# Output projection as seven block products over summed weights, with x tiles of equal rows

## The chip, the cores and the metric

The kernel runs on one core of a Trainium2 chip. The metric is the device time of one launch in microseconds (us). Most of the work is TensorE's (PE in the profile, PEld for its weight loads); VectorE (DVE) and ScalarE (ACT) prepare operands and evacuate results, GpSimd (POOL) and SyncE (SP) issue transfers.

## The reference

One layer of a hybrid encoder, 512 tokens and 16 learned meta tokens, width 2048, all in float32:

```python
hn = rmsnorm(h, norm_pre_w)
proj = hn @ w_in                       # 2048 -> z, xbc, dt, q, k, v, gate
y   = rmsnorm_groups(ssd(conv(xbc), dt) * silu(z))     # 2048 columns
att = banded_sink_attention(q, k, v) * silu(g_att)     # 1024 columns
out = concat([y, att]) @ w_out         # (512 x 3072) @ (3072 x 2048)
h = h + rmsnorm(out, norm_post_w)
```

The change concerns the last product, `out`, and what leads up to it.

## The kernel before

Every large product is made in float32 by splitting each operand into a rounded part and a remainder (`hi` and `lo` for weights, `mh` and `ml` or `xh` and `xl` for activations) and adding three matmuls: hi with high, hi with low, lo with high. A weight chunk of 128 x 1024 numbers (512 KB) is loaded by SP into a tile `st` (two of them), cast to `hi` by ScalarE (L132) and subtracted to `lo` by VectorE (L133), three tiles of each. `use(n)` on L137 asks for chunk n: it splits up to chunk n+2 and loads ahead of that. A tile of `hi` can be written again only when the matmuls of the chunk three before it are done.

The program has three stages. In the input projections (L157) 68 column tiles are multiplied, each with two chunks; the normalised x lies transposed in 16 tiles `xh[k]` and 16 `xl[k]`, grouped by four k with rows of 640, 576, 544 and 528 numbers (`X_ROW`), of which 528 are used. The 32 projections without meta tokens read 512 columns, the others two pieces of 272 (or 260) and 256. First come keys, values, and eight pairs of query and gate projections with the attention (`attend`, L512) between them; then eight groups with convolution and state-space work. Work between projections is written as generators: `yield d` means that the next part is emitted d us of estimated TensorE time later. A scheduler turns the emitted program into one order per engine, and each engine runs its own in that order; it may place a ready instruction or DMA far ahead of its place in the code.

The output projection (L853 to L905) goes over four column blocks of 512. Each takes 12 weight chunks; a chunk serves 24 matmuls (two k tiles, four token tiles, three terms), 4 x 12 x 24 = 1152 in all, each with 512 columns. Activations are split once (`splitting`, L779). A finished block is squared by ScalarE (`ojk`, L894) and weighted by VectorE (L895) straight from PSUM; after the last block `finish` (L839) takes the root and its reciprocal, and for each token tile adds the residual (L850) and stores four blocks.

Of the kernel before, what the change touches and what calls it, by code (L numbers as in the profile page):

```python
# [7 lines left out]
F32 = mybir.dt.float32  # L8
F32R = mybir.dt.float32r
# [18 lines left out]
NST = 2  # L28

X_ROW = (640, 576, 544, 528)  # L30
# [13 lines left out]
def hybrid_layer(ctx, tc, x, pre, npre, w_in, w_dt, par, w_out, npost, cst, out):  # L44
    nc = tc.nc

    def sb(name, bufs=1, **kw):
        return tc.tile_pool(name=name, bufs=bufs, **kw)
# [13 lines left out]
    def bank(pool, name):  # L62
        return pool.tile([P, 512], F32, tag="b", name=name)
# [6 lines left out]
    cw = cpool.tile([P, 32, 4], F32, name="cw")  # L70
# [39 lines left out]
    NCH = NCI + 4 * (NKO // 2)  # L110
    staged, ready = {}, {}
    nload, nsplit = [0], [0]

    def load(upto):
        while nload[0] < min(upto, NCH):
            n = nload[0]
            st = wpool.tile([P, 1024], F32, tag="st", bufs=NST, name=f"st{n}")
            if n < NCI:
                src = w_in[n // 2, :, 1024 * (n % 2):1024 * (n % 2 + 1)]
            else:  # L120
                src = w_out[(n - NCI) // (NKO // 2), (n - NCI) % (NKO // 2)]
            nc.sync.dma_start(st, src)
            staged[n] = st
            nload[0] += 1
# [58 lines left out]
    with sb("pro", side="right") as pp:  # L183
# [116 lines left out]
        with tc.manual_schedule(engines={ET.PE, ET.Activation, ET.DVE, ET.Pool}):  # L300
# [59 lines left out]
            nc.vector.tensor_scalar(cw.rearrange("p a b -> p (a b)"), pr[:, P_CW:P_CW + P], 0.5, None, ALU.mult)  # L360
# [25 lines left out]
    def steps():  # L386
# [42 lines left out]
        en = sp.tile([P, P], F32, name="en")  # L429
# [5 lines left out]
        ec = sp.tile([P, P], F32, name="ec")  # L435
# [37 lines left out]
    def keys(t, pieces):  # L473
        kr = ap.tile([P, T], F32, tag="kr", bufs=1, name=f"kr{t}")
        rope(pieces, kr, f"k{t}")
        for hh in range(2):
            src = kr[64 * hh:64 * hh + 64, :]
            g = 2 * t + hh
            own = kh[64 * hh:64 * hh + 64, g, :]
            for half in (hh, 1 - hh):  # L480
                rows = slice(64 * half, 64 * half + 64)
                nc.scalar.activation(kh[rows, g, :], src, AF.Copy, scale=0.125)
            for half in range(2):
                rows = slice(64 * half, 64 * half + 64)
                nc.vector.scalar_tensor_tensor(kl[rows, g, :], src, 0.125, own.bitcast(F32),
                                               ALU.mult, ALU.subtract)
# [14 lines left out]

    keys(0, pieces0)
# [9 lines left out]
    def attend(hp, pieces):  # L512
# [10 lines left out]
        yield 10.0  # L523
# [34 lines left out]
        yield 9.0  # L558
# [36 lines left out]
        m = mapool.tile([P, S], F32, tag="m", bufs=8, name=f"ma{hp}")  # L595
        nc.vector.scalar_tensor_tensor(m, av, 0.5, gates[hp], ALU.mult, ALU.mult)
        mix[hp] = m
# [12 lines left out]
    ub = [vpool.tile([P, T + 3], F32, name=f"ub{i}") for i in range(2)]  # L610
# [22 lines left out]
    pools = {}  # L633
# [54 lines left out]
    def unit_task(u_, xs, cT):  # L688
# [84 lines left out]
        nc.vector.reciprocal(sq, sq)  # L773
        for v, yt in ((u_ - 1, y0), (u_, yy)):
            m = pools["y"].tile([P, S], F32, tag="m", bufs=16, name=f"my{v}")
            nc.vector.scalar_tensor_tensor(m, yt, hw[:, v:v + 1], sq, ALU.mult, ALU.mult)
            mix[8 + v] = m

    def splitting(ks):  # L779
        for k in ks:  # L780
            mh[k] = o_pool(k).tile([P, S], F32R, name=f"mh{k}")
            ml[k] = o_pool(k).tile([P, S], F32R, name=f"ml{k}")
            nc.scalar.copy(mh[k], mix[k])  # L783
            nc.vector.tensor_tensor(ml[k], mix[k], mh[k].bitcast(F32), ALU.subtract)
# [31 lines left out]
    mh, ml = [None] * NKO, [None] * NKO  # L816
    vpool.release()
    xpool.release()
    o1 = ctx.enter_context(sb("o1", reuse_waits="tile"))
    o2 = []  # L820
    xr = [None] * NT

    def o_pool(k):
        if k < 16:
            return o1
        if not o2:
            assert not tasks
            pools["s"].release()
            o2.append(tc.alloc_tile_pool(name="o2", bufs=1, side="right", reuse_waits="tile"))
        return o2[0]  # L830

    with tc.high_priority(offset=400):
        splitting([0, 1])
    npw = ssq = None
    ot = {}
    n3 = None
    NC = NKO // 2

    def finish(t, jk):  # L839

        b = 3
        rs = o1.tile([P, 2], F32, tag="ors", bufs=4, name=f"ors{t}")
        nc.vector.tensor_reduce(rs[:, 0:1], ssq[:, t, 0:3], AX.X, ALU.add)
        nc.vector.tensor_scalar(rs[:, 0:1], rs[:, 0:1], 1.0 / D, EPS, ALU.mult, ALU.add)
        nc.scalar.activation(jk, pss[t], AF.Square, accum_out=ssq[:, t, 3:4])
        nc.scalar.activation(rs[:, 1:2], ssq[:, t, 3:4], AF.Sqrt, bias=rs[:, 0:1], scale=1.0 / D)
        nc.vector.tensor_tensor(ot[b, t], pss[t], npw[:, b * 512:(b + 1) * 512], ALU.mult)
        nc.vector.reciprocal(rs[:, 1:2], rs[:, 1:2])
        for b in range(4):
            nc.vector.scalar_tensor_tensor(ot[b, t], ot[b, t], rs[:, 1:2], xr[t][b], ALU.mult, ALU.add)  # L850
            nc.sync.dma_start(out[t * P:(t + 1) * P, b * 512:(b + 1) * 512], ot[b, t])

    for r in range(4):  # L853
        b = r
        toks = range(NT)
        pool = wk if b % 2 else pj
        pss = {t: bank(pool, f"po{b}_{t}") for t in toks}
        order = []
        last = 3 if r == 3 else 1
        for c in range(NC - last):  # L860
            order += [(c, kk, t) for kk in range(2) for t in toks]
        order += [(c, kk, t) for t in toks for c in range(NC - last, NC) for kk in range(2)]
        held = {}
        for c, kk, t in order:
            if c not in held:
                held[c] = use(NCI + r * NC + c)
                if r == 0 and 2 * c + 3 < NKO:
                    splitting([2 * c + 2, 2 * c + 3])
            hi, lo = held[c]
            k = 2 * c + kk  # L870
            cs = slice(t * P, (t + 1) * P)
            wh, wl = hi[:, kk * 512:(kk + 1) * 512], lo[:, kk * 512:(kk + 1) * 512]
            if n3 is None and nload[0] == NCH and b == 3:
                n3 = xr[3] = []
                for b2 in range(2):
                    xq = wpool.tile([P, 1024], F32, tag="st", bufs=NST, name=f"xr3_{b2}")
                    nc.sync.dma_start(xq, x[3 * P:, b2 * 1024:(b2 + 1) * 1024])
                    xr[3] += [xq[:, 0:512], xq[:, 512:1024]]
            for i, (a, w_) in enumerate(((mh, wh), (mh, wl), (ml, wh))):
                nc.tensor.matmul(pss[t], a[k][:, cs], w_, start=(k == 0 and i == 0), stop=(k == NKO - 1 and i == 2))  # L880
            tick(0.648)
            if k == NKO - 1:
                if npw is None:
                    npw = o1.tile([P, D], F32, name="npw")
                    ssq = o1.tile([P, NT, 4], F32, name="ssq")
                    nc.sync.dma_start(npw, npost.partition_broadcast(P))
                mp, nb = (mapool, 8) if b < 2 else (pools["y"], 16)
                o = mp.tile([P, S], F32, tag="m", bufs=nb, name=f"o{b}_{t}")
                jk = o1.tile([P, S], F32, tag="jk", bufs=1, name=f"ojk{b}_{t}")
                ot[b, t] = o  # L890
                if b == 3:
                    finish(t, jk)
                    continue
                nc.scalar.activation(jk, pss[t], AF.Square, accum_out=ssq[:, t, b:b + 1])  # L894
                nc.vector.tensor_tensor(o, pss[t], npw[:, b * 512:(b + 1) * 512], ALU.mult)  # L895
        if r == 2:
            xr[0] = o1.tile([P, D], F32, name="xr0")
            nc.sync.dma_start(xr[0], x[0:P, :])
            xr[0] = [xr[0][:, b2 * 512:(b2 + 1) * 512] for b2 in range(4)]
            for t in (1, 2):  # L900
                xr[t] = []
                for b2 in range(4):
                    xq = pools["y"].tile([P, S], F32, tag="m", bufs=16, name=f"xr{t}_{b2}")
                    nc.sync.dma_start(xq, x[t * P:(t + 1) * P, b2 * 512:(b2 + 1) * 512])
                    xr[t].append(xq)  # L905
    o2[0].release()
# [70 lines left out]
```

## Time and profile before

| | |
|---|---|
| time, median of 3 runs | 1207.39 us (1205.78 to 1208.28) |
| the profiled execution | 1206.65 us, of which its span 1204.9 us |
| mean granted TensorE clock | 0.998 |
| busy: PE / DVE / ACT / POOL | 99% / 56% / 37% / 4% of the span |
| DMA | 125.5 MB, mean 104 GB/s |

Busy time of PE overlaps between one matmul and the next, so its pace is read from the starts of matmuls, not from their lengths. DMA share is the mean busy share of 16 DMA engines. A window's row names its stretch, its length, and for each engine the busy us and the number of instructions.

### The profile page before, as it was taken

The numbers are of one execution on the slowest core, as the hardware profiler recorded it, in microseconds if no ns is written. First come the engines' busy times: TensorE is split into PE (matmuls) and PEld (weight loads), VectorE is DVE, ScalarE is ACT, GpSimd is POOL, SyncE is SP. The second block draws the span as 40 slices with busy tenths as digits, with TensorE's granted clock in tenths as the row PEclk, the third lists the DMA queues.
The fourth block names the chain that finished last, engine by engine and source line by source line (L and its number), as shares of the span: only waits on it lengthen the run. The fifth ranks groups of instructions, "written<-read, shape, count | busy, mean of one in ns | idle before, by whom it ended". The sixth has DMA issues, their size and how long they took to land.

```text
span 1204.9 us, 18243 instructions
## 1 busy us (share of the span) xinstructions
PE 1192.1 (99%) x7565; PEld 1058.1 (88%) x7565; DVE 676.4 (56%) x1196; ACT 442.8 (37%) x754; POOL 48.5 (4%) x84
## 2 busy tenths in 40 slices
PE   8999999999999999999999999999999999999997
PEld 6998888888999989999999899998998788888886
DVE  7655555555556766656658557576675922222325
ACT  7544544445422423424234233242332712121212
POOL 0000000000100001010000000100100000000000
PEclk9999999999999999999999999999999999999999
DMA  6332222222323233233333232323332423233534
GB/s 228 100 97 88 71 86 73 71 76 91 115 95 111 91 106 99 96 108 104 105 98 97 95 116 88 114 86 105 109 97 70 157 88 104 92 101 94 169 101 179
DMA packets 37045, 125.53 MB, mean 104 GB/s; under 512 B 4706, under 2 KB 5346, under 8 KB 36706
## 3 DMA queue, kind: packets, MB, share of 16 engines
q1 hardware_dynamic: 32864, 111.78, 28.5%
q0 software_dynamic: 4096, 12.59, 3.3%
q8 instruction: 59, 0.97, 0.3%
q14 instruction: 24, 0.19, 0.1%
q10 hardware_dynamic: 2, 0.01, 0.0%
HBM read 120.03 MB, written 4.33 MB: 103 GB/s over the span
## 4 chain that ended last, share of the span: by engine, by line
PE 98%; DMA 1%; DVE 0%; ACT 0%; SPq 0%; issue 0%; DVEq 0%
PE pa L157 48%; PE po L880 22%; PE pb L157 17%; PE yd L722 1%; PE av L590 1%; PE stp L732 1%; PE yo L745 1%; PE ptp L572 1%; PE xt L228 1%; PE sc L542 1%; PE cbp L649 1%; DMA x<-in_x 1%; PE xp L702 1%; PE sc L541 1%; PE stp L730 1%; PE warm L278 0%
## 5 line engine op out<-in xcount | busy, mean ns | idle before, releaser
L133 DVE TENSOR_TENSOR lo<-st,hi 128x1024 fp32r<-128x1024 f32 x182 | 222.7, 1224 | 379.9 <-ACT hi L132 376.7
L157 PE MATMUL pa<-xh,hi 128*128 128x272 f32 (+2 forms) x1088 | 374.7, 344 | 0.0
L157 PE MATMUL pa<-xl,hi 128*128 128x272 f32 (+2 forms) x1088 | 366.1, 336 | 0.0
L157 PE MATMUL pa<-xh,lo 128*128 128x272 f32 (+2 forms) x1088 | 365.8, 336 | 0.0
L132 ACT CAST hi<-st 128x1024 fp32r<-128x1024 f32 x182 | 191.4, 1052 | 471.6 <-PE po L880 169.0
L157 PEld LDWEIGHTS pa<-xh,hi 128*128 128x128 f32 x1088 | 205.5, 189 | 24.5 <-issue 3.9
L157 PEld LDWEIGHTS pa<-xh,lo 128*128 128x128 f32 x1088 | 205.4, 189 | 21.4
L157 PEld LDWEIGHTS pa<-xl,hi 128*128 128x128 f32 x1088 | 205.3, 189 | 19.0
L157 PE MATMUL pb<-xh,lo 128*128 128x256 f32 x576 | 162.6, 282 | 0.0
L157 PE MATMUL pb<-xl,hi 128*128 128x256 f32 x576 | 162.4, 282 | 0.0
L157 PE MATMUL pb<-xh,hi 128*128 128x256 f32 x576 | 162.3, 282 | 0.0
L880 PE MATMUL po<-hi,mh 128*128 128x512 f32 x384 | 149.5, 389 | 1.2 <-ACT mh L783 1.2
L880 PE MATMUL po<-lo,mh 128*128 128x512 f32 x384 | 149.4, 389 | 0.0
L880 PE MATMUL po<-hi,ml 128*128 128x512 f32 x384 | 148.9, 389 | 0.0
L157 PEld LDWEIGHTS pb<-xh,hi 128*128 128x128 f32 x576 | 108.5, 188 | 1.1
L157 PEld LDWEIGHTS pb<-xl,hi 128*128 128x128 f32 x576 | 108.4, 188 | 0.0
L157 PEld LDWEIGHTS pb<-xh,lo 128*128 128x128 f32 x576 | 108.4, 188 | 0.0
L880 PEld LDWEIGHTS po<-hi,mh 128*128 128x128 f32 x384 | 72.1, 188 | 16.2 <-ACT mh L783 1.4
L880 PEld LDWEIGHTS po<-lo,mh 128*128 128x128 f32 x384 | 72.1, 188 | 15.0
L880 PEld LDWEIGHTS po<-hi,ml 128*128 128x128 f32 x384 | 72.1, 188 | 15.0
L626 DVE SCALAR_TENSOR_TENSOR cv<-ub,cw,cv 128x528 f32<-128x528 f32 (+1 forms) x96 | 73.4, 764 | 2.4
L627 ACT ACTIVATE ct<-cv 128x528 f32<-128x528 f32 (+1 forms) x32 | 20.5, 641 | 67.1 <-DVE cv L626 67.0
(210 smaller groups left out, 1067.6 us busy)
## 6 DMA issues: line engine op xcount, KB each, us to landing
st<-in_w_in SPq DMA_DIRECT2D x136, 512.0 KB, 3.7
st<-in_w_out SPq DMA_DIRECT2D x48, 512.0 KB, 3.5
R<-scr POOLq DMA_DIRECT2D x32, 256.0 KB, 3.6
x<-in_x SPq DMA_DIRECT2D x8, 512.0 KB, 9.4
ev<-scr POOLq DMA_DIRECT2D x32, 128.0 KB, 3.0
out<-o SPq DMA_DIRECT2D x16, 256.0 KB, 2.4
xr<-in_x SPq DMA_DIRECT2D x8, 256.0 KB, 6.6
npw<-in_npost SPq DMA_DIRECT2D x1, 1024.0 KB, 4.4
```

The costliest lines, as they stand in the source:

```text
L132: nc.scalar.copy(hi, st)
L133: nc.vector.tensor_tensor(lo, st, hi.bitcast(F32), ALU.subtract)
L157: nc.tensor.matmul(ps, wt, xt[k][:, a:b], start=(k == 0 and j == 0), stop=(k == NKT - 1 and j == 2))
L228: nc.tensor.transpose(tp[:, kk, :], xts[j][:, k * P:(k + 1) * P], ident)
L541: nc.tensor.matmul(sv[:, c, o0:o1], lq, kh[:, kv, t0:t0 + o1 - o0], start=True, stop=False)
L542: nc.tensor.matmul(sv[:, c, o0:o1], lq, kl[:, kv, t0:t0 + o1 - o0], start=False, stop=True)
L572: nc.tensor.transpose(tp[:, sl * P:(sl + 1) * P], src, ident)
L590: nc.tensor.matmul(av[h * 64:h * 64 + 64, j * P:(j + 1) * P], lt, rh, start=(s_ == 0), stop=(s_ == 1))
L626: nc.vector.scalar_tensor_tensor(d, uu[:, tap + c0:tap + T], cw[:, ct, tap:tap + 1], d, ALU.mult, ALU.add)
L627: nc.scalar.activation(th[:, 0:n], d, AF.Tanh)
L649: nc.tensor.matmul(cbp[:, j * P:(j + 1) * P], bT[:, cs], cT[:, cs], start=True, stop=True)
L880: nc.tensor.matmul(pss[t], a[k][:, cs], w_, start=(k == 0 and i == 0), stop=(k == NKO - 1 and i == 2))
```

## The change

The output product is cut into a 2 x 2 block form (256 tokens x 1536 rows of weights x 1024 columns) and made with seven block products in place of eight. Four of the seven use sums of weight blocks. These are formed by a new generator `weight_sums` during the attention: in 24 steps it loads four pieces of 256 KB through GpSimd's queue, makes four additions of 128 x 512 on VectorE and stores four pieces of 256 KB to a scratch tensor `wsum` in DRAM, with two sets of tiles borrowed from the convolution. The four matching operands of the activations are combined by VectorE in `sums` and `held`, and split afresh for each product. Results are combined in `done`. Two waits in `attend` grow (10 to 12, 9 to 11). All x tiles get rows of 576 numbers (2304 bytes); a copy of the convolution weights (512 bytes) is dropped.

```diff
-X_ROW = (640, 576, 544, 528)
+X_ROW = 576
...
-    NCH = NCI + 4 * (NKO // 2)
+    NCH = NCI + 7 * KH                       # KH = 12 chunks a product
+    wsum = dpool.tile([4, 2, KH // 2, P, 1024], F32, name="wsum")
+    W_SRC = [w_block(0, 0), wsum[1], w_block(1, 0), wsum[0], wsum[2], w_block(1, 1), wsum[3]]
...
+            if n % 4 > 1 and "o" in pools:
+                st = pools["o"].tile([P, 1024], F32, tag="st", bufs=2, name=f"st{n}")
...
-        load(n + 3 + NST)
+        load(n + 3 + (4 if "o" in pools else NST))
...
+        def fetch(n):
+            tags = (("cT", 2), ("xs", 2), ("th", 1) if n % 2 else ("bT", 1))
+            v = [vpool.tile([P, T], F32, tag=tag, bufs=bufs, name=f"ws{n}_{m}") for m, (tag, bufs) in enumerate(tags)]
+            sets[n] = [t[:, 0:512] for t in v + [ub[n % 2]]]
+            for to, fr in zip(sets[n], (w22, w12, w11, w21)):
...
+                nc.gpsimd.dma_start(to, fr[at(n)])
+        fetch(0)
+        yield 5.0
+        for n in range(2 * KH):
+            if n + 1 < 2 * KH:
+                fetch(n + 1)
+            td, tb_, ta, tc_ = sets.pop(n)
+            for m, to, other in ((2, td, tb_), (0, tb_, ta), (1, ta, td), (3, tc_, ta)):
+                nc.vector.tensor_tensor(to, to, other, ALU.add)
+                nc.gpsimd.dma_start(wsum[m][at(n)], to)
+            yield 9.8
+    spawn(weight_sums(), 6.0)
...
-        yield 10.0
+        yield 12.0
...
-        yield 9.0
+        yield 11.0
...
+    def sums(i):                              # six pairs of k tiles
+        nc.vector.tensor_tensor(s1[i], h2[:, :, HI], h1[:, :, HI], ALU.subtract)
+        nc.vector.tensor_tensor(s2[i], s1[i], h1[:, :, LO], ALU.add)
+    def held(p, i):
+        if p == 1:
+            sums(i)
+        elif p == 4:
+            nc.vector.tensor_tensor(h1[:, :, HI], h1[:, :, LO], h1[:, :, HI], ALU.subtract)
+        elif p == 5:
+            nc.vector.tensor_tensor(s2[i], s2[i], h2[:, :, LO], ALU.subtract)
+        src = (h1[:, :, LO], s2[i], h2[:, :, LO], s1[i], h1[:, :, HI], s2[i], h2[:, :, HI])[p]
+        ah = o1.tile([P, 2, 256], F32R, tag="ah", bufs=9, name=f"ah{p}_{i}")
+        al = o1.tile([P, 2, 256], F32R, tag="al", bufs=9, name=f"al{p}_{i}")
+        nc.scalar.copy(ah, src)
+        nc.vector.tensor_tensor(al, src, ah.bitcast(F32), ALU.subtract)
...
+    def weigh(t, b, src):
+        nc.scalar.activation(jk, src, AF.Square, accum_out=ssq[:, t, n:n + 1])
+        nc.vector.tensor_tensor(oo[t, b], src, npw[:, b * 512:(b + 1) * 512], ALU.mult)
+    def done(p, t, b, ps):
+        if p == 0:   ...  nc.scalar.copy(oo[t, b], ps)
+        elif p == 1: ...  nc.vector.tensor_tensor(uu[t, b], ps, oo[t, b], ALU.subtract)
+        elif p == 2:
+            nc.vector.tensor_tensor(c, ps, c, ALU.add)
+            weigh(t, b, c)
+        elif p == 3: ...  nc.vector.tensor_tensor(vv[t, b], uu[t, b], ps, ALU.subtract)
+        elif p == 4:
+            nc.vector.tensor_tensor(c, vv[t, b], ps, ALU.subtract)
+            nc.vector.tensor_tensor(uu[t, b], ps, uu[t, b], ALU.subtract)
+            weigh(t + 2, b + 2, c)
+        elif p == 5:
+            nc.vector.tensor_tensor(c, c, ps, ALU.subtract)
+            weigh(t, b + 2, c)
+            if b == 1:
+                finish(t, 3)
+        else:
+            nc.vector.tensor_tensor(c, ps, c, ALU.add)
+            weigh(t + 2, b, c)
+            if b == 1:
+                finish(t + 2, 1)
...
+    for p in range(7):                        # a chunk: one b, two token tiles, two kk, three terms
+        order = [(i, t) for i in range(KH - last) for t in range(2)]
+        order += [(i, t) for t in range(2) for i in range(KH - last, KH)]
```

## Rows read from the trace of the kernel before

**Rows 1.** The page: busy times of the engines, and the chain by engine

```profile
PE 1192.1 (99%) x7565; PEld 1058.1 (88%) x7565; DVE 676.4 (56%) x1196; ACT 442.8 (37%) x754; POOL 48.5 (4%) x84
...
PE 98%; DMA 1%; DVE 0%; ACT 0%; SPq 0%; issue 0%; DVEq 0%
```

**Rows 2.** Windows: attention, start of the output projection, its rest, the end

```profile
45.00:336.00 291.00, 291.00 (x1843) 252.12 (x1841) 159.17 (x354) 143.02 (x317) 4.36 (x8) 1.00 0.27 86
...
933.80:967.00 33.20, 31.95 (x142) 26.32 (x142) 29.66 (x39) 21.67 (x35) 0.00 (x0) 1.00 0.43 145
967.00:1197.10 230.10, 230.10 (x1016) 190.39 (x1015) 68.01 (x78) 53.06 (x73) 0.00 (x0) 1.00 0.35 113
1197.10:1204.90 7.80, 0.18 (x1) 0.00 (x0) 3.89 (x7) 0.98 (x3) 0.00 (x0) 0.74 0.63 234
```

**Rows 3.** The chain in order of time, output projection: start, us, what

```profile
934.80 0.53 ACT mh L783
...
947.72 249.57 PE po L880 x1101
```

**Rows 4.** Timeline of PE, one projection of 512 columns: k = 2, 9, 15

```profile
500.90 0.39 PE L157 MATMUL pa<-xh,hi 128*128 128x512 f32 x1
...
505.67 0.40 PE L157 MATMUL pa<-xh,hi 128*128 128x512 f32 x1
...
509.84 0.39 PE L157 MATMUL pa<-xh,hi 128*128 128x512 f32 x1
```

**Rows 5.** Groups of instructions: busy us, mean ns, idle before them

```profile
L133 DVE TENSOR_TENSOR lo<-st,hi 128x1024 fp32r<-128x1024 f32 x182 | 222.7, 1224 | 379.9 <-ACT hi L132 376.7 <-PE ptp L572 2.7
...
L132 ACT CAST hi<-st 128x1024 fp32r<-128x1024 f32 x182 | 191.4, 1052 | 471.6 <-PE po L880 169.0 <-PE pb L157 167.1 <-PE pa L157 67.5
...
L773 DVE RECIPROCAL rs<-rs 128x512 f32<-128x512 f32 x8 | 26.8, 3346 | 0.0
...
L850 DVE SCALAR_TENSOR_TENSOR o<-o,ors,xr 128x512 f32<-128x512 f32 x16 | 11.0, 748 | 0.1
```

**Rows 6.** Timeline of VectorE, one head pair of the attention

```profile
164.40 1.84 DVE L557 TENSOR_SCALAR pbuf<-pbuf,sm 128x80 f32<-128x80 f32 x8
...
170.91 0.41 DVE L565 COPY pm<-ptm 16x256 f32<-16x256 f32 x1 [0.16 <-PE ptm L563]
...
182.13 1.41 DVE L522 TENSOR_TENSOR qs<-qr,qs 64x512 fp32r<-64x512 f32 x2
...
187.51 0.46 DVE L546 TENSOR_REDUCE mx<-sc 128x1 f32<-128x80 f32 x2 [1.73 <-PE sc L542]
```

**Rows 7.** Timelines of ScalarE and VectorE in the output projection

```profile
985.15 1.05 ACT L132 CAST hi<-st 128x1024 fp32r<-128x1024 f32 x1 [4.38 <-PE po L880]
...
986.24 1.23 DVE L133 TENSOR_TENSOR lo<-st,hi 128x1024 fp32r<-128x1024 f32 x1 [4.21 <-ACT hi L132]
...
944.59 3.10 DVE L784 TENSOR_TENSOR ml<-my,mh 128x512 fp32r<-128x512 f32 x5
```

**Rows 8.** Timeline of SP: two loads emitted after the first and third block

```profile
933.26 0.33 SPq L886 DMA_DIRECT2D npw<-in_npost  x1
...
936.72 0.43 SPq L898 DMA_DIRECT2D xr<-in_x  x1
```

**Rows 9.** DMA issues (KB each, median us to landing), and POOL's group for one

```profile
R<-scr POOLq DMA_DIRECT2D x32, 256.0 KB, 3.6
x<-in_x SPq DMA_DIRECT2D x8, 512.0 KB, 9.4
...
L674 POOL DMA_DIRECT2D R<-scr x32 | 18.0, 565 | 328.7 <-DVE swq L470 291.7 <-PE yd L722 29.2 <-ACT pbuf L550 7.8
```

**Rows 10.** Window of the first loads, with the DMA engines full

```profile
9.00:14.00 5.00, 3.70 (x11) 1.79 (x11) 4.13 (x7) 4.15 (x10) 0.00 (x0) 1.00 1.02 410
```

**Rows 11.** Timelines of ScalarE and VectorE at the end

```profile
1197.31 0.60 ACT L845 ACTIVATE ojk<-po 128x512 f32<-128x512 f32 x1 [3.06 <-PE po L880]
...
1198.83 2.74 DVE L850 SCALAR_TENSOR_TENSOR o<-o,ors,xr 128x512 f32<-128x512 f32 x4
```

More of the change, by code (lines that the diff above doesn't have):

```diff
@@ L500, in values, with weight_sums, at @@
         nc.vector.tensor_copy(vm[:, t * P:(t + 1) * P], tq[0:NM, 0:P])
+    ub = [vpool.tile([P, T + 3], F32, name=f"ub{i}") for i in range(2)]
+    def weight_sums():
+        w11, w12, w21, w22 = [w_block(r, q) for r in range(2) for q in range(2)]
+        sets = {}
+        def at(n):
+            return n // 2 % 2, n // 4, slice(None), slice(512 * (n % 2), 512 * (n % 2) + 512)
+        def fetch(n):
[3 more added lines that the diff above has]
+            for to, fr in zip(sets[n], (w22, w12, w11, w21)):
+                if n < 2:
+                    tc.keep_in_program_order(nc.vector.memset(to[:, 0:1], 0.0))
+                nc.gpsimd.dma_start(to, fr[at(n)])
[10 more added lines that the diff above has]
+    spawn(weight_sums(), 6.0)
     keys(0, pieces0)
@@ L773, in unit_task @@
         nc.vector.reciprocal(sq, sq)
+        mix[4 + g] = pools["y"].tile([P, 2, S], F32, tag="m", bufs=8, name=f"my{g}")
         for v, yt in ((u_ - 1, y0), (u_, yy)):
[L775 to L784, printed above, removed]
+            nc.vector.scalar_tensor_tensor(mix[4 + g][:, v % 2], yt, hw[:, v:v + 1], sq, ALU.mult, ALU.mult)
     for g in range(8):
@@ L834, in hybrid_layer @@
[L834 to L870, printed above, removed]
-            cs = slice(t * P, (t + 1) * P)
[L872 to L905, printed above, removed]
@@ L906, in hybrid_layer @@
-    o2[0].release()
+    pools["o"] = o1 = ctx.enter_context(sb("o1", reuse_waits="tile"))
+    LO, HI = slice(0, 256), slice(256, 512)
+    NP = KH // 2
+    s1, s2 = [None] * NP, [None] * NP
+    def sums(i):
+        h1, h2 = mix[i], mix[NP + i]
+        s1[i] = o1.tile([P, 2, 256], F32, name=f"s1_{i}")
+        s2[i] = o1.tile([P, 2, 256], F32, name=f"s2_{i}")
+        nc.vector.tensor_tensor(s1[i], h2[:, :, HI], h1[:, :, HI], ALU.subtract)
+        nc.vector.tensor_tensor(s2[i], s1[i], h1[:, :, LO], ALU.add)
@@ new lines, in hybrid_layer, with o_tile @@
+    ops = {}
+    with tc.high_priority(offset=400):
+        ops[0] = held(0, 0)
+    npw = o1.tile([P, D], F32, name="npw")
+    nc.sync.dma_start(npw, npost.partition_broadcast(P))
+    ssq = o1.tile([P, NT, 4], F32, name="ssq")
+    uu, vv, oo, xr, rs = {}, {}, {}, {}, {}
+    def o_tile(name):
+        return pools["c"].tile([P, S], F32, name=name)
+    def weigh(t, b, src):
+        n = b if t < 2 else (0, 3, 1, 2)[b]
+        jk = o1.tile([P, S], F32, tag="jk", bufs=1, name=f"jk{t}_{b}")
+        nc.scalar.activation(jk, src, AF.Square, accum_out=ssq[:, t, n:n + 1])
+        nc.vector.tensor_tensor(oo[t, b], src, npw[:, b * 512:(b + 1) * 512], ALU.mult)
@@ new lines, in residual, with finish @@
+    def residual(t):
+        pool, nb = (mapool, 4) if t < 2 else (pools["y"], 8)
+        for h in range(2):
+            xq = pool.tile([P, 2, S], F32, tag="m", bufs=nb, name=f"xr{t}_{h}")
+            nc.sync.dma_start(xq.rearrange("p a b -> p (a b)"), x[t * P:(t + 1) * P, h * 1024:(h + 1) * 1024])
+            xr[t, 2 * h], xr[t, 2 * h + 1] = xq[:, 0], xq[:, 1]
+    def finish(t, last):
+        nc.scalar.activation(rs[t][:, 1:2], ssq[:, t, 3:4], AF.Sqrt, bias=rs[t][:, 0:1], scale=1.0 / D)
+        nc.vector.reciprocal(rs[t][:, 1:2], rs[t][:, 1:2])
+        for b in [b for b in range(4) if b != last] + [last]:
+            nc.vector.scalar_tensor_tensor(oo[t, b], oo[t, b], rs[t][:, 1:2], xr[t, b], ALU.mult, ALU.add)
+            nc.sync.dma_start(out[t * P:(t + 1) * P, b * 512:(b + 1) * 512], oo[t, b])
@@ new lines, in hybrid_layer @@
+    tb = [(t, b) for t in range(2) for b in range(2)]
+    for p in range(7):
+        pss = {v: bank((pj, wk)[p % 2], f"po{p}_{v[0]}{v[1]}") for v in tb}
+        last = 3 if p == 6 else 1
+        order = [(i, t) for i in range(KH - last) for t in range(2)]
+        order += [(i, t) for t in range(2) for i in range(KH - last, KH)]
+        wts = {}
+        for i, t in order:
+            if i not in wts:
+                wts[i] = use(NCI + p * KH + i)
+                if i % 2 == 0:
+                    n = p * NP + i // 2
+                    for m in range(n + 1, min(n + 3, 7 * NP)):
+                        if m not in ops:
+                            ops[m] = held(m // NP, m % NP)
+                if p == 5 and i in (0, 2):
+                    residual(i // 2)
+                if p == 6 and i in (2, 4):
+                    residual(1 + i // 2)
+            hi, lo = wts[i]
+            ah, al = ops[p * NP + i // 2]
+            b = i % 2
+            cs = slice(t * P, (t + 1) * P)
+            for kk in range(2):
+                ws = slice(kk * 512, (kk + 1) * 512)
+                for j, (a, w_) in enumerate(((ah, hi), (ah, lo), (al, hi))):
+                    nc.tensor.matmul(pss[t, b], a[:, kk, cs], w_[:, ws], start=(i < 2 and kk == 0 and j == 0),
+                                     stop=(i >= KH - 2 and kk == 1 and j == 2))
+                tick(0.68)
+            if i >= KH - 2:
+                done(p, t, b, pss[t, b])
```

68 lines of the change are left out of this document (44 added, 24 removed).

## The prediction, made before the changed kernel was run

> **What bounds the kernel now.** I read the page first: TensorE is busy 99% of the span and 98% of the chain that ended last [rows 1], so only a change in TensorE's stream, or a new wait of it, can move the time. Then the windows, to see what room the helpers have in each stage: VectorE is busy 159.2 of 291 us in the attention, where the DMA engines are 27% busy, and 68.0 of 230.1 us in most of the output projection, but 29.7 of 33.2 us at its start [rows 2]. Then the chain in order of time: 1101 output matmuls in a row take 249.57 us, 0.2267 us each, with no break [rows 3]. Last the timelines, for slack.
>
> **Fewer matmuls.** Before: 4 blocks x 12 chunks x 24 = 1152. After: 7 products x 12 chunks x 12 = 1008. 144 x 0.2267 = **-32.6 us** [rows 3]. The form (128 x 128 stationary, 512 columns moving) is unchanged, so the pace should be.
>
> **x tiles.** In one undisturbed projection the 7 steps from k = 2 to k = 9 take 4.77 us (21 matmuls, 227.1 ns each), the 6 from k = 9 to k = 15 take 4.17 us (18 matmuls, 231.7 ns) [rows 4]. The quick ones lie in rows of 2560 and 2304 bytes and the first row of the 2176 ones; the slow ones are k = 9 to 15 and, as the starts of the 32 projections of 512 columns show, k = 0 and 1, which follow them in time. I read this as the tile row's size mattering: 2304, 2560 are multiples of 256, 2176 and 2112 are not, and it takes a few matmuls to recover. Uniform 2304 would make all quick: 32 x 9 k x 3 x 4.6 ns = -4.0 us. The projections in two pieces show no gain by k. Bounds: 0 if the row is not the cause; +3.1 (32 x 7 x 3 x 4.6 ns) if all became slow. I take **-3.5**.
>
> **Weight sums in the attention.** 24 steps of 4 additions, 128 x 512 each. The nearest row is five `ml` subtractions of that size in 3.10 us, 0.62 us each [rows 7]: 96 x 0.62 = 59.5 us of VectorE. It is hidden if the 131.8 us that VectorE idles there [rows 2] can be used: load goes from 55% to 75%. The eight memsets of the first two sets, at 0.2 us or so, go the same way. What the additions can delay is the chain of a head pair. `qs` ends at 183.54 and the maximum over scores begins at 187.51 behind its matmuls; the normalisation ends at 166.24 and its transposes are consumed from 170.91 [rows 6]. So some 4 us of slack at either place, and the longer yields add 2 to each. One burst of four additions is 2.5 us: it fits. The weights' split has more: two chunks of 24 matmuls, 10.9 us, for 2.3 us of work [rows 7]. The later scores cost nothing themselves, as the same matmuls move behind others; the last head pair ends some 4 us later, with the first group's projections to cover it.
>
> Each step moves 8 x 256 KB, 2.1 MB, by 8 issues of GpSimd at 0.565 us [rows 9], 4.5 us of an engine that is idle there. At 9.8 us a step that is 214 GB/s beside the 86 GB/s of now [rows 2], 300 together; the first loads reached 410 [rows 10]. It fits, but the scheduler may run it faster than its yields say: `npw` and `xr`, emitted after the first and third block, were issued at 933.26 and 936.72 [rows 8]. At 6.5 us a step the demand would be 409, all there is. Then an addition stands at the head of VectorE's queue until its pieces land, with the weights' split and the scores queued behind it and TensorE waiting for those. Bounds 0 to 71 (rival 1). I take **+2**, since a 256 KB load lands 3.6 us after its issue [rows 9] and is asked for a step ahead.
>
> **The output stage.** A chunk now serves 12 matmuls, 2.72 us in place of 5.44, and `hi` of chunk n+2 can only start when chunk n-1 is done. From there cast and subtraction take 2.32 us (985.15 to 987.47) [rows 7] and have 5.44: slack 3.1 us. A product lasts 32.6 us. VectorE has in it: 12 `lo` x 1.224 [rows 5] = 14.7; 6 `al` x 0.62 = 3.7; sums, 7.4 in product 1, 3.7 in products 4 and 5, if not made ahead; and the combining of the product before, 0 / 2.5 / 5.0 / 2.5 / 7.4 / 10.5 us at the start of products 1, 2, 3, 4, 5, 6 (4, 8, 4, 12, 8 operations x 0.62; the last with 8 residual additions at 0.685, from 2.74 us for four [rows 11]). The heaviest are product 5 (29.5) and 6 (28.9): 90%. ScalarE needs 12 x 1.05 + 6 x 0.53 [rows 3, 5] = 16 us and some squares. So both keep up on average, and only bursts in front of a `lo` stall TensorE:
> - Product 0 begins while the last state-space unit ends: a reciprocal of 3.35 us [rows 5] and two products behind it, 4.7 us, against 3.1 of slack. Bounds 0 to 1.6; **+1**.
> - Products 4 to 5: 7.4 us of combining in two halves, half of it before the last chunk: **+0.5** (0 to 4.3).
> - Products 5 to 6: after the last two blocks VectorE has 2 x 1.2 of combining and weighting and 2 x 2.74 of residuals, some 8 us, with hand-overs to ScalarE in which a `lo` can slip in. `lo` of chunk 2 slips in; that of chunk 3, due at 8.2, comes at about 10.5: **+2.5** (0 to 5.7).
>
> Loads of 512 KB every 2.72 us are 193 GB/s, under half of 410 [rows 10], and with four `st` tiles they are asked for some 8 us ahead: nothing. The first wait for ScalarE's `mh` (0.53 us in the chain [rows 3]) stays as wait for `ah`.
>
> **The end.** Now the square starts on PSUM when the last matmul ends (1197.31) and the last four residual additions start at 1198.83 [rows 11]. After it, one addition from PSUM goes first: **+0.7**.
>
> **Sum.** Against the profiled execution, 1206.65 us (span 1204.9 and 1.75 around it): -32.6 - 3.5 + 2 + 1 + 0.5 + 2.5 + 0.7 = -29.4, so 1177.2. The median of the runs shown is 0.74 above that execution; I give **1178.0** as median.
>
> **Rivals.**
> 1. *Slower: VectorE waits for pieces.* The additions leave 131.8 - 59.5 = 72 us idle, 3.0 a step. If pieces land as the queued `x` loads do, 9.4 us after issue [rows 9], and the scheduler counted on 3.6, each step holds VectorE 5.8 us: (5.8 - 3.0) x 24 = 67 us on TensorE, 1243. It decides from a wait of 3.0 + 29.4/24 = 4.2 us a step. For it: the full queue above. Against: the stage has 291 us and the sums need only 50.3 MB / 324 GB/s = 155.
> 2. *The attention chain is late by bursts.* If three bursts (7.5 us) fall in a slack of 6, 1.5 us is lost for 8 head pairs, or at both places: 12 to 24 us, 1188 to 1200.
> 3. *GpSimd's issues are held by VectorE.* If they can't proceed while VectorE runs instructions like L557, a set comes up to 1.84 us late once in each head pair [rows 6]: 8 x 1.84 = 14.7 us, 1191. Against: the 32 issues of `R`, made while VectorE was busy with such instructions too, took 0.565 us each [rows 9]. The Trainium skill (SBUF — State Buffer, section "SBUF: two separate sides") says that descriptors of a DMA issued from GpSimd can't be written while VectorE holds the shared port pair in a two-port mode, and speaks against moving 192 transfers to that queue; by that rule 1191, by the row 1178.
> 4. *Bursts stall all heavy product changes.* If no `lo` slips in, the changes cost 5.7, 4.3 and 1.9 (products 5, 4, 2), and ScalarE's squares 1 each: some 15 in place of 3, 1190.
> 5. *No change*: only a mixture with some 29 us of stalls.
>
> **Chances.** Forecast 1170 to 1186: 0.62. Rival 1: 0.09 (0.02 of it within 0.2% of before, 0.07 slower). Rival 2: 0.12. Rival 3: 0.04. Rival 4: 0.10. Faster than 1170: 0.03. Two in ten may fall out; 1169 to 1195 leaves out rival 1 and the upper part of rival 2, some 0.15, with a little below. 0.2% (2.4 us) is about what these runs can tell from no change. Faster 0.90, same 0.03, slower 0.07.
>
> **What would show it.** Right: 1008 matmuls of the output at 0.227 us; k = 9 to 15 at 227 ns; `wsum` stores ending before 336; no wait of PE on L133 or L132 in the attention; waits of 1 to 3 us at the start of products 5 and 6. Wrong: VectorE's additions waiting for DMA by more than 3 us each, PE waiting for `sc`, `ptp` or `lo` many times, an output stage longer than 240 us, or slow x tiles at rows of 2304 bytes.

## The result, and the profile after

The changed kernel takes 1257.83 us (median of 4 runs, 1255.25 to 1259.2), against 1207.27 us (1205.78 to 1208.28) for the kernel before, timed with it: a ratio of 1.0421, 95% interval 1.0406 to 1.0435. It is slower by 50.6 us, where 29 us less were forecast. The profiled execution took 1257.08 us, with a span of 1255.2 and a mean granted clock of 0.969.

Three starts of matmuls cut the span into stages: the first `cbp` (the first state-space product, which ends the attention stage), the first `po` and the last `po` of the output stage.

| us | before | after | difference |
|---|---|---|---|
| start to first `cbp` | 341.7 | 421.6 | +79.9 |
| first `cbp` to first `po` | 593.7 | 591.7 | -2.0 |
| first to last `po` | 261.5 | 230.9 | -30.6 |
| last `po` to the end | 8.0 | 10.9 | +2.9 |
| span | 1204.9 | 1255.2 | +50.3 |

The output stage gave what it should, but for 2 us of breaks, and the attention stage took 80 us more. The page of the changed kernel, busy times and the granted clock in 40 slices (a 9 is full speed):

```profile
PE 1182.8 (94%) x7421; PEld 1048.8 (84%) x7421; DVE 820.9 (65%) x1406; ACT 491.8 (39%) x812; POOL 151.8 (12%) x276
...
PEclk9999878889999999999999999999999999999998
```

TensorE is no longer busy all the time [rows 1], and slices five to nine show a lower clock. Windows of the changed kernel: the attention in pieces, first, then the output stage (its first product, the rest, the end):

```profile
100.00:150.00 50.00, 34.88 (x144) 28.68 (x143) 30.25 (x58) 16.27 (x35) 21.47 (x40) 0.84 0.86 279
150.00:200.00 50.00, 37.04 (x169) 29.92 (x169) 30.70 (x60) 14.51 (x34) 25.80 (x48) 0.78 0.84 283
200.00:250.00 50.00, 39.09 (x217) 31.50 (x216) 27.49 (x56) 15.74 (x35) 21.45 (x40) 0.90 0.81 268
...
300.00:340.00 40.00, 40.00 (x222) 33.29 (x221) 21.92 (x50) 19.76 (x46) 0.00 (x0) 1.00 0.25 80
...
1013.00:1046.00 33.00, 32.64 (x144) 27.04 (x145) 32.89 (x41) 21.01 (x29) 0.00 (x0) 1.00 0.63 210
1046.00:1244.40 198.40, 197.14 (x868) 162.27 (x866) 145.47 (x176) 101.05 (x135) 0.00 (x0) 1.00 0.64 210
1244.40:1255.20 10.80, 0.28 (x2) 0.00 (x0) 6.94 (x14) 1.74 (x5) 0.00 (x0) 0.61 0.52 194
```

The attention ran with no break of TensorE before [rows 2]; between 100 and 250 us TensorE is now busy 35 to 39 of each 50 us, and VectorE, at 27 to 31 of 50, is not full either. As soon as the sums are done (POOL at 0 in 300 to 340) everything is as before. What VectorE waits for between 60 and 290 us, then TensorE between 60 and 425, then GpSimd (total, times, longest):

```profile
DVE ws L544 <- DMA ws<-in_w_out: 70.3, 31, 5.7
DVE ws L544 <- DMA wsum<-ws: 8.3, 3, 3.7
```

```profile
PE ptp L619 <- DVE pm L612: 12.4, 2, 6.6
PE sc L588 <- DVE qs L569: 12.1, 2, 8.2
PE ptm L610 <- DVE pbuf L604: 11.0, 2, 8.5
PE av L637 <- DVE pm L612: 5.1, 2, 3.1
```

```profile
POOL ws L534 <- DMA wsum<-ws: 97.0, 28, 6.5
```

A chain of three waits can be read from them. GpSimd stands before a fetch until the stores from the same tiles have landed; VectorE stands in an addition (L544) until a fetched piece has landed; TensorE stands until VectorE has made something of the attention that is queued behind the addition. One place in VectorE's timeline:

```profile
129.83 0.69 DVE L544 TENSOR_TENSOR ws<-ws,ws 128x512 f32<-128x512 f32 x1 [3.99 <-DMA ws<-in_w_out]
130.81 1.42 DVE L544 TENSOR_TENSOR ws<-ws,ws 128x512 f32<-128x512 f32 x2 [0.28 <-DMA ws<-in_w_out]
...
136.05 0.69 DVE L544 TENSOR_TENSOR ws<-ws,ws 128x512 f32<-128x512 f32 x1
136.66 0.62 DVE L593 TENSOR_REDUCE mx<-sc 128x1 f32<-128x192 f32 x2
140.95 0.69 DVE L544 TENSOR_TENSOR ws<-ws,ws 128x512 f32<-128x512 f32 x1 [3.68 <-DMA wsum<-ws]
141.56 0.22 DVE L594 TENSOR_SCALAR ng<-mx,pr 128x2 f32<-128x2 f32 x1
```

At 136.66 the maxima over scores are made, but the small instruction that finishes them (L594) stands behind an addition that waits, and comes 4 us later. (The profile puts that wait down to a store, but the piece that the same addition waits for, fetched at 133.50, landed at 140.83, just before it.) The Trainium skill (PSUM — Partial Sum Buffer, section "Engine vs sequencer instructions") says that the queues of ScalarE, VectorE and GpSimd are strictly first in, first out; this timeline agrees, with those 4 us.

DMA issues (KB each, median us from issue to landing), and GpSimd's time for one issue (ns, shortest, median, longest):

```profile
ws<-in_w_out POOLq DMA_DIRECT2D x72, 256.0 KB, 4.1
wsum<-ws POOLq DMA_DIRECT2D x72, 256.0 KB, 6.4
```

```profile
L545 POOL DMA_DIRECT2D wsum<-ws x72: 539/546/597, 65.7 to 281.9; - x72
```

The stores land in 6.4 us. An issue takes 0.546 us, as `R` did before [rows 9].

### The profile page after: what moved, and what is told of

It is laid out like the page before. It is cut to its first block, busy times and chain, and to the rows that moved or that the text cites. A ratio compares the mean times of both kernels' runs of the same rounds, so it can differ in the third digit from the quotient of the medians.

```text
span 1255.2 us, 18787 instructions
## 1 busy us (share of the span) xinstructions
PE 1182.8 (94%) x7421; PEld 1048.8 (84%) x7421; DVE 820.9 (65%) x1406; ACT 491.8 (39%) x812; POOL 151.8 (12%) x276
## 5 line engine op out<-in xcount | busy, mean ns | idle before, releaser
L147 DVE TENSOR_TENSOR lo<-st,hi 128x1024 fp32r<-128x1024 f32 x218 | 266.0, 1223 | 195.5 <-ACT hi L146 194.7
L146 ACT CAST hi<-st 128x1024 fp32r<-128x1024 f32 x218 | 228.7, 1050 | 390.5 <-PE pb L171 173.1
L994 PE MATMUL po<-lo,ah 128*128 128x512 f32 x336 | 131.1, 390 | 1.3 <-DVE lo L147 1.3
L994 PE MATMUL po<-hi,ah 128*128 128x512 f32 x336 | 129.7, 389 | 1.2 <-ACT ah L886 1.2
L994 PE MATMUL po<-hi,al 128*128 128x512 f32 x336 | 130.3, 389 | 0.0
L544 DVE TENSOR_TENSOR ws<-ws,ws 128x512 f32<-128x512 f32 x72 | 49.7, 690 | 79.3 <-DMA ws<-in_w_out 70.3
L994 PEld LDWEIGHTS po<-lo,ah 128*128 128x128 f32 x336 | 63.1, 188 | 15.5 <-DVE lo L147 2.4
L994 PEld LDWEIGHTS po<-hi,ah 128*128 128x128 f32 x336 | 63.1, 188 | 14.5 <-ACT ah L886 1.4
L673 DVE SCALAR_TENSOR_TENSOR cv<-ub,pr,cv 128x528 f32<-128x528 f32 (+1 forms) x96 | 73.4, 764 | 2.4
L994 PEld LDWEIGHTS po<-hi,al 128*128 128x128 f32 x336 | 63.1, 188 | 12.9
```

What stands on the lines that cost most here:

```text
L146: nc.scalar.copy(hi, st)
L147: nc.vector.tensor_tensor(lo, st, hi.bitcast(F32), ALU.subtract)
L544: nc.vector.tensor_tensor(to, to, other, ALU.add)
L673: nc.vector.scalar_tensor_tensor(d, uu[:, tap + c0:tap + T], cw[:, ct, tap:tap + 1], d, ALU.mult, ALU.add)
L994: nc.tensor.matmul(pss[t, b], a[:, kk, cs], w_[:, ws], start=(i < 2 and kk == 0 and j == 0), stop=(i >= KH - 2 and kk == 1 and j == 2))
```

## The experiments

Each ran on one chip beside the kernel before. Experiments 3, 6, 7 and 8 are one run each; for the others the time is the median of 4 to 6 runs, and every other column is from the profiled one alone. "TensorE idle" is the sum of its gaps, "low clock" the time at a granted clock of 0.5 (1.2 GHz), both from 45 us to the first `cbp`, summed from the trace. The columns "additions" give the start of the first and of the last.

| | time, us | first `cbp` | TensorE idle | low clock | additions |
|---|---|---|---|---|---|
| before | 1207.27 | 341.7 | 0 | 0 | none |
| after | 1257.83 | 421.6 | 56.0 | 68.3 | 64.7 to 281.6 |
| 1 first addition pinned | 1194.96 | 360.0 | 14.2 | 17.1 | 66.3 to 327.7 |
| 2 no sums | 1176.17 | 340.7 | 0.1 | 0 | none |
| 3 no additions | 1251.1 | 415.5 | 70.8 | 71.7 | none |
| 4 x rows alone | 1203.51 | 340.6 | 0 | 0 | none |
| 5 pinned, early pads | 1182.86 | 347.8 | 4.6 | 6.8 | 74.5 to 318.6 |
| 6 no stores | 1201.93 | 366.3 | 17.2 | 20.5 | 66.4 to 194.4 |
| 7 no additions, early pads | 1178.15 | 341.9 | 0.6 | 0 | none |
| 8 early pads alone | 1254.72 | 419.1 | 53.8 | 68.3 | 65.5 to 281.0 |
| 9 as 5, second step later | 1189.28 | 346.7 | 4.3 | 6.8 | 74.1 to 314.1 |
| 10 as 9, other order at the end | 1187.1 | 348.9 | 5.1 | 3.4 | 75.6 to 316.6 |

**1. The first addition of each step kept in program order.**

```diff
-                nc.vector.tensor_tensor(to, to, other, ALU.add)
+                add = nc.vector.tensor_tensor(to, to, other, ALU.add)
+                if m == 2:
+                    tc.keep_in_program_order(add)
```

> The changed kernel, with the first addition of each of the 24 steps pinned behind what is emitted before it on VectorE, so that a step's additions stand in the queue at the 9.8 us that the code asks for, and not every 5.5 to 6 us where the scheduler put them. Nothing else differs. Theory A (the additions stand in VectorE's queue sooner than two sets of tiles can be loaded, added, stored and loaded again, some 9 us a step, and what is behind them comes late): VectorE's waits for landed pieces fall from 83 us to under 15, the first cbp matmul comes back from 421 to about 345, the time is 1172 to 1190. Theory B (the stage is short of something itself: 50 MB of transfers beside the weights, or 60 us more on VectorE): 24 steps at any place cost much the same, the time stays above 1230.

1194.96 us (1193.91 to 1195.49), 0.9898 of before (0.9885 to 0.9912). One line that only fixes where the additions stand in VectorE's queue gives back 63 of the 81 us that the sums cost (experiment 2 has the base). The steps now come every 10.9 us ((327.7 - 66.3) / 24), and VectorE's waits for pieces fall from 70.3 to 4.1 us. What stays lost lies at the two ends. At the start TensorE waits for `tr` in `steps`, whose `acs` stands behind the first additions. At the end VectorE stands for 8.4 us around the memset of a pad of `ub` (the profile names no releaser), and then TensorE waits 7.9 us for `pm`, which VectorE makes only behind the additions of the last two steps. TensorE's timeline at the start, its wait at the end (total, times, longest), and VectorE's timeline there:

```profile
77.17 0.33 PE L454 MATMUL tr<-ident,acs 128*128 128x128 f32 x1 [1.23 <-DVE acs L438]
82.52 0.48 PE L455 MATMUL tr<-ident,ec 128*128 128x128 f32 x1 [5.02 <-ACT ec L451]
```

```profile
PE ptp L621 <- DVE pm L614: 7.9, 1, 7.9
```

```profile
313.72 0.23 DVE L595 TENSOR_REDUCE mx<-sc 128x1 f32<-128x80 f32 x1 [8.38 <-issue]
313.74 0.06 DVE L661 MEMSET ub<- 128x3 f32 x1
...
330.45 0.41 DVE L614 COPY pm<-ptm 16x256 f32<-16x256 f32 x1 [2.01 <-issue]
```

**2. No sums.** The generator isn't started and the output stage reads plain blocks of `w_out` in place of sums (another output).

```diff
-    W_SRC = [w_block(0, 0), wsum[1], w_block(1, 0), wsum[0], wsum[2], w_block(1, 1), wsum[3]]
+    W_SRC = [w_block(0, 0), w_block(0, 1), w_block(1, 0), w_block(0, 1), w_block(1, 0), w_block(1, 1), w_block(0, 0)]
...
-    spawn(weight_sums(), 6.0)
```

> The changed kernel with no weight sums: the generator is not started, and the four products that want sums read plain blocks of the weights (the output is another one). It keeps the seven products, the longer yields and the x tiles. Theories A and B alike: the attention is back to its old length, the output stage stays at 231 us, so 1257.8 - 80 = about 1176. If the yields or the combining of activations were part of the loss: above 1185, with the first cbp matmul later than 345.

1176.17 us (1175.02 to 1176.99), 0.9743 (0.973 to 0.9756): all of the change but the sums is worth 31.2 us, and the whole loss is in the sums, 1255.2 - 1174.6 = 80.6 us of span.

**3. The transfers without the 96 additions** (another output).

```diff
-                nc.vector.tensor_tensor(to, to, other, ALU.add)
```

> The changed kernel without the 96 additions: all pieces are still loaded and stored (the scratch tensor holds plain weights, so the output is another one). Theory A: nothing on VectorE waits for a landing, so TensorE has no breaks in the attention and the time is 1173 to 1182, though the same 50 MB move. Theory B in the form that the transfers crowd out the weights' own loads: most of the loss stays, above 1230, with ScalarE's casts waiting for st.

1251.1 us: nearly no better, and the expectation of the theory is missed. But the loss has another form. VectorE's waits between 60 and 300 us have one entry for a DMA, and its timeline shows where:

```profile
DVE ub L658 <- DMA ub<-in_w_out: 75.9, 1, 75.9
```

```profile
274.16 0.06 DVE L658 MEMSET ub<- 128x3 f32 x1 [75.86 <-DMA ub<-in_w_out]
```

A memset of 0.06 us, that of the pad which the convolution needs later, was put into VectorE's queue 76 us ahead of the end of the transfers that share its tile, and held everything behind it. TensorE had no break before that one. This gave a narrower theory: any VectorE instruction that waits for these transfers and stands too early in the queue is the cause, be it an addition or a memset; the transfers as such are not.

**4. The kernel before with x rows of 2304 bytes.**

```diff
-X_ROW = (640, 576, 544, 528)
+X_ROW = 576
...
-    cw = cpool.tile([P, 32, 4], F32, name="cw")
+    cw = pr[:, P_CW:P_CW + P].rearrange("p (a b) -> p a b", b=4)
```

> The kernel before with only the x tiles at rows of 576 numbers (and the copy of the convolution weights dropped, which makes the room). If the row size sets the pace: all k at 227 ns for three times 16 matmuls, 4.1 us less, 1203.2. If it is where the tile lies, or other work at that time: within 1 us of 1207.3.

1203.51 us (1201.92 to 1204.29), 0.9966 (0.9954 to 0.9978), 3.9 us less. The edit changes the length of the rows and with it the place where each row begins.

**5. Pinned, the pads zeroed before the sums, the first step later, 9.2 in place of 9.8 asked for a step.**

```diff
     ub = [vpool.tile([P, T + 3], F32, name=f"ub{i}") for i in range(2)]
+    for t in ub:
+        nc.vector.memset(t[:, 0:3], 0.0)
...
-            sets[n] = [t[:, 0:512] for t in v + [ub[n % 2]]]
+            sets[n] = [t[:, 0:512] for t in v] + [ub[n % 2][:, 3:515]]
...
-        yield 5.0
+        yield 15.0
...
-            yield 9.8
+            yield 9.2
```

> The first addition of each step stays in program order, the conv tiles' pads are zeroed once before the sums (which now use columns 3 to 514 of ub), the first step comes 10 us later and a step is asked for every 9.4 in place of 9.8. Theory (VectorE's in-order queue is what stalls, wherever an instruction stands that waits for a transfer): the two losses of the pinned kernel, at 77 to 82 us and around 305 to 335 us, go, some 14 us of 19; 1176 to 1183 us, faster than both kernels. Rival (the pinned kernel's remaining loss is the additions' own time on VectorE, or the full DMA engines delaying other loads): it stays at 1190 to 1197. If the shorter step is more than the DMA engines carry, VectorE's waits for ws come back, with some 1 us a step, 1200.

(The figure of 9.4 in that text is a slip: the kernel asks for 9.2.) 1182.86 us (1180.3 to 1185.49), 0.9802 (0.9787 to 0.9817): faster than both kernels. Both breaks of experiment 1 are gone (idle time 14.2 to 4.6 us); as the edits were made together, the run does not tell which removed which. One new break stands near the start of the sums; VectorE, then TensorE:

```profile
104.59 0.69 DVE L546 TENSOR_TENSOR ws<-ws,ws 128x512 f32<-128x512 f32 x1 [5.81 <-DMA ws<-in_w_out]
```

```profile
112.50 0.41 PE L592 MATMUL sc<-kh,qs 128*128 128x80 f32 x1 [4.34 <-DVE qs L573]
```

**6. The additions without the stores**, pads early (another output; plain blocks as in experiment 2).

```diff
                 nc.vector.tensor_tensor(to, to, other, ALU.add)
-                nc.gpsimd.dma_start(wsum[m][at(n)], to)
```

> As the changed kernel, with the loads and all 96 additions where they are, but nothing is stored to wsum, and the output stage reads plain blocks of w_out in place of the sums (so the output is another); pads zeroed before the sums. Theory (the round of two sets, whose length the stores' landing sets, is what the additions wait for): without the stores a set is free when its additions are done, a step takes 6 us or less, the scheduler's pace, and VectorE's waits go nearly away: 1174 to 1190 us. Rival (96 additions in bursts, or loads on GpSimd's queue as such, delay the attention): 1230 to 1255.

1201.93 us, between the two: 366.3 - 340.7 = 25.6 us are lost with no store at all. A step takes 5.4 us, (194.4 - 66.4) / 24. The window with most of it, and VectorE's waits for pieces:

```profile
100.00:150.00 50.00, 43.35 (x232) 35.18 (x230) 45.91 (x84) 19.44 (x40) 21.15 (x40) 0.99 0.85 285
```

```profile
DVE ws L546 <- DMA ws<-in_w_out: 19.6, 15, 3.3
```

VectorE is busy 45.9 of 50 us there: additions, weight split and attention together nearly fill it, and it still waits 19.6 us for pieces. So the theory was half right: without stores a step is short, but crowding costs something too. How much of the changed kernel's loss is crowding can't be read from this run, as its order is another one. Between the first additions of the first and the last step stand 15 weight splits in VectorE's queue here, and 20 in the changed kernel, so the scheduler set the steps closer still.

**7. Transfers without additions, pads early** (another output).

```diff
-                nc.vector.tensor_tensor(to, to, other, ALU.add)
```

with the pad edits of experiment 5.

> All 192 transfers, none of the 96 additions (the stored blocks are unsummed, so the output is another), and the pads zeroed before the sums, so that no VectorE instruction waits for a transfer of the sums. Theory: transfers alone cost TensorE nothing; 1174 to 1182 us, and the single wait of 75 us is gone. Rival (the wait was only the place where a lack of DMA capacity showed): a stall of 30 to 75 us remains elsewhere, at the first conv tiles or at the weights' loads, 1205 to 1250.

1178.15 us: the 75.9 us are gone. All 192 transfers together cost the attention stage 341.9 - 340.7 = 1.2 us. A window in the midst of them:

```profile
200.00:250.00 50.00, 50.00 (x298) 41.72 (x297) 25.11 (x56) 24.68 (x60) 23.08 (x43) 1.00 0.94 315
```

TensorE is without a break at full clock while the DMA engines are 94% busy. ScalarE's casts, which wait 32.1 us for weight loads in the attention of the changed kernel, wait 1.2 us here: those waits came with the stalls, not with the transfers.

**8. The changed kernel with early pads alone** (the pad edits of experiment 5, nothing else).

> The changed kernel with only the pads zeroed before the sums, additions placed by the scheduler. Theory: the additions hold VectorE's queue all along, so the pad was no part of the changed kernel's loss: 1245 to 1262 us. Rival (the pad's memset carries part of the loss, as with the additions left out): under 1235.

1254.72 us, with the first `cbp` 2.5 us earlier than in the changed kernel. In the changed kernel the pad plays next to no part, as there the additions hold the queue already.

**9. As 5, with the second step later.**

```diff
-            yield 9.2
+            yield 9.2 if n else 14.0
```

> As the kernel with pinned additions and early pads, with 14.0 in place of 9.2 asked for behind the first step alone. In that kernel the second step began 6.1 us behind the first, the stores of the first set had not landed when its next fetch was due, the fourth step waited 5.8 us for a piece at 98.8 us, and TensorE stood 4.3 us for qs at 108.2 us, with 6.8 us of half clock behind it. Theory (each wait of VectorE for a piece comes from two steps nearer than the round of two sets allows): that break goes, 4 to 7 us less: 1176 to 1180 us. Rival (the DMA engines are full there, and the wait only moves to a later step): 1181 to 1185.

1189.28 us (1182.34 to 1193.7), 0.9843 (0.9816 to 0.9869): a miss, of the theory and of its rival. The break at 108 us did go, but another came where the last transfers meet the first convolution. TensorE's longest wait, and what ScalarE had waited for there:

```profile
PE av L641 <- ACT pt L626: 2.5, 1, 2.5
```

```profile
317.11 0.38 ACT L669 COPY ub<-pa 128x260 f32<-128x260 f32 x1 [4.04 <-DMA wsum<-ub]
```

The five runs are 11 us apart, those of experiment 2 are 2 us apart. The profiled one is the shortest, so what the longer ones lost is not in a trace.

**10. As 9, with an addition of the last token tile ahead of three residual additions at the end.** `put` is the loop of residual additions and stores, taken out of `finish`.

```diff
-            if b == 1:
-                finish(t + 2, 1)
+            if t == 0 and b == 1:
+                scale(2)
+            elif t == 1 and b == 0:
+                put(2, (0, 2, 3, 1))
+            elif t == 1:
+                scale(3)
+                put(3, (0, 2, 3, 1))
```

> As the kernel before it, and at the end the first addition of token tile 3 goes ahead of the last three residual additions of token tile 2, so that its last two additions from PSUM no longer stand behind four residual additions. Theory (the end is longer than before because of VectorE's order there): the time from the start of the last output matmul to the end falls from 10.9 to 8.9 to 9.6 us, the whole by 1.3 to 2.0 us against the kernel without this edit. Rival (the end is set by the last four residual additions and the stores behind them alone): 10.9 stays.

1187.1 us (1182.76 to 1191.86); the end stays at 10.9 us from the last `po`. One addition went ahead, but the last one now stands behind the weighting and the residuals; VectorE:

```profile
1173.45 0.74 DVE L931 SCALAR_TENSOR_TENSOR u<-u,ors,xr 128x512 f32<-128x512 f32 x1
1174.11 0.15 DVE L936 TENSOR_REDUCE ors<-ssq 128x1 f32<-128x3 f32 x1
1174.18 0.68 DVE L974 TENSOR_TENSOR u<-po,u 128x512 f32<-128x512 f32 x1
```

Reordering moved the wait, and did not shorten it.

## Why the prediction was wrong, point by point

**Fewer matmuls: right.** The chain of the changed kernel, in the output stage:

```profile
1025.00 155.05 PE po L994 x684
```

That is 0.2267 us each, as before [rows 3]. 1008 of them are 228.5 us of the 230.9. The 2.4 us left are breaks, where 4 were allowed: by the starts of matmuls some 0.6 in product 0 (the kernel before has as much there), 1.0 early in product 5 and 0.9 early in product 6. In the group of `po` matmuls, waits for `lo` are 1.3 us in total and for `ah` 1.2. Rival 4 did not happen.

**x tiles: the size right, the cause narrowed but not settled.** Experiment 4 gives 3.9 us (2.7 to 5.6 by its interval) against a term of 3.5 and a full effect of 4.0. The starts of k = 2, 9 and 15 in one projection of the changed kernel:

```profile
580.33 0.40 PE L171 MATMUL pa<-xh,hi 128*128 128x512 f32 x1
...
585.11 0.39 PE L171 MATMUL pa<-xh,hi 128*128 128x512 f32 x1
...
589.19 0.39 PE L171 MATMUL pa<-xh,hi 128*128 128x512 f32 x1
```

18 matmuls from k = 9 to k = 15 in 4.08 us are 226.7 ns each; they were 231.7 [rows 4]. Two points of the reading don't hold up. k = 0 was counted among the nine k that would become quick, and stays slow: 231.3 ns before, 231.2 in experiment 4 (medians over the 32 projections, from the starts of matmuls), while k = 1 goes from 232.0 to 228.0. So eight k gained and not nine, and that 3.9 lies so near 4.0 is in part chance. And k = 8 was quick before (226.7), though it lies in rows of 2176 bytes: it is the first row of its tile. Since longer rows also move the starts of the rows, that the row's length counts, and not where it begins, is not shown.

**Weight sums in the attention: the step that failed.** +2 was taken; by experiment 2 the stage pays 421.6 - 340.7 = 80.9 us. 55.9 of them are time in which TensorE stood. The other 25.0 are what it worked more slowly: it was at a granted 0.5 (1.2 GHz) for 68.3 us, in stretches that come with its breaks and go with them in experiments 2 and 7. It was at work in 49.5 of the 68.3, and half of that is 24.8. Three readings were wrong in the step.

*The pace.* 24 steps at 9.8 us each were taken as the plan, with "the scheduler may run it faster" as a risk. The order of VectorE's queue shows what was really asked for: the 20 weight splits that stand between the first additions of the first and the last step take 130.1 us in experiment 2 (67.3 to 197.4), where TensorE has no breaks, so 5.7 us a step (130.1 / 23). At that pace the forecast 59.5 us of additions are not spread over 291 us but over some 130, and VectorE's room there, 45% of it or 59 us, is gone before any piece is late. Nor can the transfers follow, by the step's own figures: 2.1 MB in 5.7 us are 368 GB/s, with 86 beside them 454, more than the 410 that it took for all there is. Experiments 1 and 5 have the same additions and the same transfers, spread over 261 and 244 us, and lose 19.3 and 7.1 us of the stage in place of 80.9.

*The round.* "A 256 KB load lands 3.6 us after its issue and is asked for a step ahead" left out what the fetch itself waits for. A set of tiles can be fetched into again only when its four stores have landed, and these took 6.4 us, a row that the trace of before did not have. Four fetch issues (2.2), landing (4.1), the four additions, four store issues (2.2) and the stores' landing (6.4) make some 18 us for a set, 9 us a step with two sets. The changed kernel ran at (281.6 - 64.7) / 24 = 9.0. So the queue asked for 5.7, the round gave 9.0, and VectorE stood for the difference: 78.6 us of waits, 3.3 a step. Without additions the transfers run at much the same 9.1 (stores from 67.8 to 286.0 in experiment 7), so the additions don't set that pace.

*The capacity.* 410 GB/s was taken for the DMA engines from the first loads [rows 10]. With these pieces, read and written, they are 94% busy at 315 GB/s (experiment 7). From that row, some 335 GB/s are all there is, and 249 of them are left beside the 86 of before: 8.4 us a step, an estimate. So whether the two sets or the engines set the 9.0 is not separated by a run. But the transfers by themselves were not what hurt: experiment 7 carries everything, 9.1 us a step, and loses 1.2 us.

**Rival 1 was the right mechanism, with a chance of 0.09.** What was held against it, that the sums need only 155 us of transfers in a stage of 291, is an average; an instruction in an in-order queue waits for its own piece, however idle the engine is over the stage. Its reason for late pieces was another one: it supposed 9.4 us from issue to landing, and the pieces landed in 4.1 (median), but were issued late, behind the stores (GpSimd's 97.0 us of waits). Its price was 67 us where TensorE stood 55.9, and it had no term for the clock, 25.0. And it was to decide from 4.2 us of wait a step, as if VectorE's idle time could take up the rest; 3.3 us a step were enough. A likely reason is that the chain of a head pair had only some 6 us of slack, by the prediction's own reading, for a burst and a wait together; no run changes that slack.

**Rival 2 is not separated from it.** Bursts without a late piece cost at most the 7.1 us of experiment 5 at its 10.2 us a step. No run has the changed kernel's pace without its waits.

**Rival 3 did not show.** By the Trainium skill (SBUF — State Buffer, section "SBUF: two separate sides") GpSimd's descriptors can wait for VectorE's two-port modes; the 72 issues of L545 took 0.539 to 0.597 us each beside a VectorE that worked between its waits, so no run here shows such a hold.

**The end: right in kind, too small.** +0.7 was taken, it is +2.9. VectorE at the end of the changed kernel:

```profile
1242.99 0.75 DVE L920 SCALAR_TENSOR_TENSOR u<-u,ors,xr 128x512 f32<-128x512 f32 x1
1243.66 1.41 DVE L920 SCALAR_TENSOR_TENSOR c<-c,ors,xr 128x512 f32<-128x512 f32 x2
1244.98 0.75 DVE L920 SCALAR_TENSOR_TENSOR u<-u,ors,xr 128x512 f32<-128x512 f32 x1
1245.64 1.28 DVE L963 TENSOR_TENSOR u<-po,u 128x512 f32<-128x512 f32 x2
...
1251.24 0.75 DVE L920 SCALAR_TENSOR_TENSOR u<-u,ors,xr 128x512 f32<-128x512 f32 x1
```

The last matmul starts at 1244.3, and the additions from PSUM come at 1245.64 behind four residual additions of the tile before. The step counted one addition more; it did not count that a token tile now leaves two additions, two weightings and four residual additions, some 5.4 us, at an end where the tiles come 4.1 us apart (18 matmuls). Experiment 10 speaks for work, not order, as one other order gave the same 10.9 us.

**What stays open.** Experiment 5 is still 6.7 us above experiment 2. Experiments 9 and 10 moved the last break and did not remove it, and why their runs lie 11 and 9 us apart was not found. Experiments 5 and 9 were timed on different occasions, and their intervals touch, so that which of them is better isn't settled.

## What to carry to other kernels

When background work with DMA-fed instructions is put beside a critical chain, an average of bytes and of busy time proves nothing: write down the round of one buffer set (fetch issue, landing, work, store issue, store landing), and compare it with the pace at which the order in the engine's queue asks for it (here 9.0 us against 5.7). Where a scheduler chooses that order, one pinned instruction a step can be worth more than the algorithm: here 63 us, against 31 for an eighth fewer output matmuls and the x tiles together. And an instruction of next to no length, such as the memset of a pad, is a barrier for its engine if its tile is lent to transfers.

## What the hardware showed that was not expected

A memset of 0.06 us held VectorE for 75.9 us, and TensorE with it for 70 (experiment 3). The pace of matmuls moved with the rows of the moving operand's tile: 231.7 ns each with rows of 2176 and 2112 bytes, 226.7 with rows of 2304, and 3.9 us of the time with that edit alone (experiment 4). And what breaks of TensorE cost beyond their own length depends on how they lie: in the changed kernel 55.9 us in many breaks came with 25.0 us of slower work at the granted 0.5, while in experiment 3 one break of 70.5 us came with some 4, as 66 of its 71.7 us at 0.5 passed while TensorE stood.
